# Row skewness on one core: a written order, slices of three and delayed copies exchanged for scheduled order, slices of two and copies at each block's end

## The chip, the cores and the metric

The kernel runs on one core of a Trainium2 chip. The metric is the device time of one execution in microseconds; the median of several executions is compared. The profile is one further execution, recorded by the hardware profiler.

## What is computed

For each of 1024 rows of 8192 float32 values the kernel returns the skewness:

```
mean = np.mean(x, axis=-1); std = np.std(x, axis=-1)
z = (x - mean) / (std + 1e-8)
out = np.mean(z ** 3, axis=-1)          # 1024 values
```

The kernel works with three sums per row, over x, x² and x³, and combines them: with S1, S2 and S3 as means, var = S2 - S1², and the result is (S3 - 3·S1·S2 + 2·S1³)·var^-1.5, which it evaluates as (S3 + (-3·S1)·(var + S1²/3))·var^-1.5 or in the equal form with S2 - (2/3)·S1².

## The kernel before, in words

The 1024 rows are eight blocks of 128 rows, one row per partition. Each block is loaded in column pieces called units (list `UNITS`, L18 to L27): blocks 0 to 3 in two units of 4096 columns, blocks 4 and 5 in three, block 6 in five, block 7 in eight small ones. All loads are issued by SyncE (L188) into a pool of eight buffers, so the ninth load and those after it wait until the buffer of the load eight places earlier has been released by its readers.

Every unit has three readers:

- ScalarE (ACT) squares it in slices, L195, with the running sum of squares as a by-product (accumulator column of `s2u`). The function `_slices` cuts a unit into parts of at most 2304 columns; units of at least 3584 columns in block 2 and later are cut into three parts of at most 1408.
- VectorE (DVE) multiplies each square by x, L200, with the sum of cubes as a by-product (column of `s3u`). It needs the square of the same slice, and the squares live in four buffers.
- TensorE (PE) transposes each 128 columns with an identity matrix and adds them up in PSUM (`tp`, L213), so that a block ends with one 128x128 matrix whose rows must still be summed. ScalarE copies it to SBUF (`copy_sums`, L112) and a matmul with a column of 1/8192 (`mean`, L115) yields the mean. In blocks 0 to 2, ScalarE sums 1024 columns of the first unit itself (L207).

The last slice of all keeps its square in PSUM (`sqps`) and its cube in another tile (`cube`).

The order on each engine is the order in which the program is written: `manual_schedule` (L52) takes the engines out of the scheduler's hands. A small table `todo`, filled by `at(b, k, fn)`, says which extra step stands after unit k of block b. The copy and the mean matmul of block b stand behind unit 0 of block b+1. The closing arithmetic of blocks 0 to 5 stands in block 6 (`first_sums`, `first_rest`), that of block 6 in block 7 (`mid_sums` L158, `mid_power` L163 to L166, `third_1` L169, `third_2` L172). The end for block 7, L223 to L241, is: copy, sum of `s2u`, mean, square of the mean, GpSimd (POOL) variance and power -1.5 (L232, L233), two Identity activations with a sum of `s3u` between them (L169, L226, L172), and one DVE operation with two per-row scalars that finishes the column (L238). Then SyncE looks at the last eight loads (L243) and stores 4 KB (L246).

Of the kernel before, what the change touches and what calls it, by code (L numbers as in the profile page):

```python
# [8 lines left out]
FP = mybir.dt.float32  # L9
AF = mybir.ActivationFunctionType  # L10
ALU = mybir.AluOpType
# [3 lines left out]
X_AXIS = mybir.AxisListType.X  # L15


UNITS = [  # L18
    [4096, 4096],
    [4096, 4096],  # L20
    [4096, 4096],
    [4096, 4096],
    [3072, 2944, 2176],
    [2944, 2688, 2560],
    [1664, 1536, 1664, 1792, 1536],
    [1024, 1152, 768, 1024, 1024, 1280, 1024, 896],
]  # L27
S1_ACT = {(0, 0): 1024, (1, 0): 1024, (2, 0): 1024}
SUB_MAX = 2304
SUB_WIDE = 1408  # L30
WIDE = 3584
X_BUFS = 8
SQ_BUFS = 4
EARLY = 6


def _slices(b, w):
    n = -(-w // (SUB_WIDE if b >= 2 and w >= WIDE else SUB_MAX))
    step = -(-w // n // 128) * 128
    return [(s, min(s + step, w)) for s in range(0, w, step)]  # L40

# [2 lines left out]
def kernel(  # L44
# [3 lines left out]
    out: bass.AP,  # L48
):
    nc = tc.nc  # L50
    eng = mybir.EngineType
    ctx.enter_context(tc.manual_schedule(  # L52
        engines={eng.PE, eng.Activation, eng.DVE, eng.Pool, eng.SP}))
    P = nc.NUM_PARTITIONS
    R, C = x.shape
    NB = R // P
    L = NB - 1
    F = EARLY
    inv_n = 1.0 / float(C)
    s_scale = float(C) ** -0.5  # L60
    third = (1.0 / 3.0) ** 0.5
    assert len(UNITS) == NB and all(sum(u) == C for u in UNITS) and F == L - 1
    nw = len(S1_ACT)
    assert sorted(b for b, _ in S1_ACT) == list(range(nw)) and nw <= F

# [2 lines left out]
    ov = out.rearrange("(p b) -> p b", b=NB)  # L68


    n_sl = [sum(len(_slices(b, w)) for w in u) for b, u in enumerate(UNITS)]
    K = max(n_sl)

    xpool = ctx.enter_context(tc.tile_pool(name="xp", bufs=X_BUFS))
    sqpool = ctx.enter_context(tc.tile_pool(name="sqp", bufs=SQ_BUFS))
# [1 line left out]
    psum = ctx.enter_context(tc.tile_pool(name="ps", bufs=2, space=bass.MemoryType.PSUM))  # L77
    psum1 = ctx.enter_context(tc.tile_pool(name="ps1", bufs=1, space=bass.MemoryType.PSUM))

    def small(name, n):  # L80
        return onep.tile([P, n], FP, tag=name, name=name)

    onesn = small("onesn", 1)
# [5 lines left out]
    s2u = small("s2u", NB * K)  # L89
    s3u = small("s3u", NB * K)  # L90
    nc.vector.memset(s2u, 0.0)
    nc.vector.memset(s3u, 0.0)
    s1a = small("s1a", nw)
    same = small("same", max(S1_ACT.values()))
    junk = small("junk", K)
    expo = small("expo", F)
    nc.gpsimd.memset(expo, -1.5)
    skew = small("skew", NB)
    s1ps = psum1.tile([P, NB], FP, tag="s1ps", name="s1ps")
    m1a = small("m1a", F)  # L100
    Tsb = [small(f"tsb{i}", P) for i in range(2)]
    tps = {}
    act, g, v = nc.scalar.activation, nc.gpsimd, nc.vector

    loads = []
    todo = {}

    def at(b, k, fn):
        todo.setdefault((b, k), []).append(fn)

    def copy_sums(b):
        nc.scalar.copy(out=Tsb[b % 2], in_=tps[b])  # L112

    def mean(b):
        nc.tensor.matmul(  # L115
            out=s1ps[:, b : b + 1], lhsT=Tsb[b % 2], rhs=onesn, start=True, stop=True
        )

    for b in range(L):
        at(b + 1, 0, lambda b=b: copy_sums(b))  # L120
        at(b + 1, 0, lambda b=b: mean(b))


    m2a, m3a, m1sqa, m1sq3a, nm1a, vara, rra = (
        small(f"{t}a", F) for t in ("m2", "m3", "m1sq", "m1sq3", "nm1", "var", "rr")
    )

    def first_sums():
        for dst, src in ((m2a, s2u), (m3a, s3u)):
            v.tensor_reduce(  # L130
                out=dst, in_=src[:, 0 : F * K].rearrange("p (b c) -> p b c", c=K),
                axis=X_AXIS, op=ALU.add,
            )
        nc.scalar.copy(out=m1a[:, nw:F], in_=s1ps[:, nw:F])
        act(out=m1sqa, in_=m1a, func=AF.Square)
        g.tensor_tensor(out=vara, in0=m2a, in1=m1sqa, op=ALU.subtract)  # L136
        g.tensor_tensor(out=rra, in0=vara, in1=expo, op=ALU.pow)  # L137

    def first_rest():
        act(out=m1sq3a, in_=m1a, func=AF.Square, scale=third)  # L140
        act(out=nm1a, in_=m1a, func=AF.Copy, scale=-3.0)
        g.tensor_tensor(out=m1sq3a, in0=m1sq3a, in1=vara, op=ALU.add)
        g.tensor_tensor(out=m1sq3a, in0=m1sq3a, in1=nm1a, op=ALU.mult)  # L143
        g.tensor_tensor(out=m3a, in0=m3a, in1=m1sq3a, op=ALU.add)  # L144
        g.tensor_tensor(out=skew[:, 0:F], in0=m3a, in1=rra, op=ALU.mult)  # L145

    at(F - 2, 0, lambda: v.tensor_tensor(  # L147
        out=m1a[:, 0:nw], in0=s1ps[:, 0:nw], in1=s1a, op=ALU.add))
    at(F, 1, first_sums)
    at(F, 2, first_rest)  # L150


    names = ("m2", "m3", "m1sq", "nm1", "var", "v3", "rr", "t")
    mid, end = ({t: small(f"{t}_{b}", 1) for t in names} for b in (F, L))

    def mid_sums():
        for t, src in (("m2", s2u), ("m3", s3u)):
            v.tensor_reduce(  # L158
                out=mid[t], in_=src[:, F * K : F * K + n_sl[F]], axis=X_AXIS, op=ALU.add
            )  # L160

    def mid_power():
        act(out=mid["m1sq"], in_=s1ps[:, F : F + 1], func=AF.Square)  # L163
        act(out=mid["nm1"], in_=s1ps[:, F : F + 1], func=AF.Copy, scale=-3.0)
        g.tensor_tensor(out=mid["var"], in0=mid["m2"], in1=mid["m1sq"], op=ALU.subtract)  # L165
        g.tensor_tensor(out=mid["rr"], in0=mid["var"], in1=expo[:, 0:1], op=ALU.pow)  # L166

    def third_1(o):
        act(out=o["v3"], in_=o["m1sq"], func=AF.Identity, scale=-2.0 / 3.0, bias=o["m2"])  # L169

    def third_2(o):
        act(out=o["t"], in_=o["v3"], func=AF.Identity, scale=o["nm1"], bias=o["m3"])  # L172

    at(L, 0, mid_sums)
    at(L, 1, mid_power)
    at(L, 4, lambda: third_1(mid))
    at(L, 5, lambda: third_2(mid))
    at(L, 5, lambda: g.tensor_tensor(  # L178
        out=skew[:, F : F + 1], in0=mid["t"], in1=mid["rr"], op=ALU.mult))

    for b, widths in enumerate(UNITS):
        tp = tps[b] = psum.tile([P, P], FP, tag="tp", name=f"tp_{b}")
        c0 = 0
        j = b * K
        for k, w in enumerate(widths):
            last_unit = b == L and k == len(widths) - 1
            xt = xpool.tile([P, w], FP, tag="x", name=f"x_{b}_{k}")
            loads.append(nc.sync.dma_start(out=xt, in_=xv[b, :, c0 : c0 + w]))  # L188
            c0 += w
            for s, e in _slices(b, w):  # L190
                if last_unit:
                    sq = psum1.tile([P, e - s], FP, tag="sqps", name="sqps")
                else:
                    sq = sqpool.tile([P, e - s], FP, tag="sq", name=f"sq_{b}_{k}_{s}")
                act(  # L195
                    out=sq, in_=xt[:, s:e], func=AF.Square, scale=s_scale,
                    accum_out=s2u[:, j : j + 1],
                )
                cube = sqpool.tile([P, e - s], FP, tag="sq", name="cube") if last_unit else sq
                v.scalar_tensor_tensor(  # L200
                    out=cube, in0=sq, scalar=1.0, in1=xt[:, s:e],
                    op0=ALU.mult, op1=ALU.mult, accum_out=s3u[:, j : j + 1],
                )
                j += 1
            w_act = S1_ACT.get((b, k), 0)
            if w_act:
                act(  # L207
                    out=same[:, 0:w_act], in_=xt[:, w - w_act : w], func=AF.Copy,
                    scale=inv_n, accum_out=s1a[:, b : b + 1],
                )  # L210
            n = (w - w_act) // P
            for c in range(n):
                nc.tensor.matmul(  # L213
                    out=tp, lhsT=xt[:, c * P : (c + 1) * P], rhs=ident,
                    start=(k == 0 and c == 0), stop=(c0 == C and c == n - 1),
                    is_transpose=True,
                )
            for fn in todo.pop((b, k), ()):
                fn()
    assert not todo  # L220


    o, p1 = end, s1ps[:, L : L + 1]  # L223

    def row_sum(out, src, n):
        act(out=junk[:, 0:n], in_=src[:, L * K : L * K + n], func=AF.Copy, accum_out=out)  # L226

    copy_sums(L)
    row_sum(o["m2"], s2u, n_sl[L])
    mean(L)  # L230
    act(out=o["m1sq"], in_=p1, func=AF.Square)  # L231
    g.tensor_tensor(out=o["var"], in0=o["m2"], in1=o["m1sq"], op=ALU.subtract)  # L232
    g.tensor_tensor(out=o["rr"], in0=o["var"], in1=expo[:, 0:1], op=ALU.pow)  # L233
    act(out=o["nm1"], in_=p1, func=AF.Copy, scale=-3.0)
    third_1(o)
    row_sum(o["m3"], s3u, n_sl[L] - 1)
    third_2(o)
    v.tensor_scalar(  # L238
        out=skew[:, L:NB], in0=s3u[:, j - 1 : j], scalar1=o["t"], scalar2=o["rr"],
        op0=ALU.add, op1=ALU.mult,  # L240
    )  # L241

    seen = nc.sync.nop()  # L243
    for ld in loads[-8:]:
# [32 lines left out]
```

## Time and profile before

| | us |
|---|---|
| Median of 4 runs | 91.13 (91.04 to 91.15) |
| The profiled execution's own time | 91.19 |
| Its span, first to last instruction | 89.4 |
| DVE busy, share of the span | 73.5, 82% |
| ACT busy | 72.6, 81% |
| PE busy | 65.5, 73% |
| POOL busy | 13.7, 15% |
| Read from HBM | 33.55 MB, 375 GB/s over the span |

The time outside the span is 1.79 us. "Idle before" of an instruction is the time its engine stood still in front of it; the arrow names what ended that. A slice on ACT or DVE is one long instruction and a short accumulator read (80 to 190 ns), which overlaps the start of the next slice: the distance between the starts of two slices is shorter than the sum of their durations.

### The profile page before, as it was taken

How to read it: one execution, taken by the hardware profiler on the slowest of the kernel's cores; microseconds unless marked ns; L12 is line 12 of the kernel's file. 1: busy time of each engine (PE TensorE's matmuls, PEld its weight loads, DVE VectorE, ACT ScalarE, POOL GpSimd, SP SyncE). 2: the span in 40 equal slices, each digit the busy share in tenths (PEclk: the TensorE clock that was granted, in tenths of full speed). 3: DMA queues.
4: the chain of work that ended last, by engine and by line, in shares of the span. 5: the costliest groups of instructions: out<-in, count | busy, mean ns of one | idle time of the engine just before them, and what ended most of it. 6: DMA issues, size and time to landing. Idle time of an engine off the chain costs nothing.

```text
span 89.4 us, 1405 instructions
## 1 busy us (share of the span) xinstructions
PE 65.5 (73%) x504; PEld 61.0 (68%) x504; DVE 73.5 (82%) x97; ACT 72.6 (81%) x120; POOL 13.7 (15%) x18
## 2 busy tenths in 40 slices
PE   0003999792797925999999699489897889897810
PEld 0003999691796915999999598479796778865710
DVE  1000498989989497999989999999999999999980
ACT  6003999599990999979799999499899989998960
POOL 3000000000000000000000000000000089999730
PEclk9999999999958997599999999999999999999999
DMA  5899999999999999999999999999999999995000
GB/s 117 337 411 425 455 425 411 455 433 411 447 440 389 455 440 396 455 418 422 425 419 401 443 420 413 427 424 408 411 419 415 418 405 405 414 410 230 10 0 2
DMA packets 4038, 33.64 MB, mean 376 GB/s; under 512 B 576, under 2 KB 576, under 8 KB 2240
## 3 DMA queue, kind: packets, MB, share of 16 engines
q1 hardware_dynamic: 4032, 33.56, 90.2%
q8 instruction: 4, 0.07, 0.3%
q14 instruction: 2, 0.02, 0.0%
HBM read 33.55 MB, written 0.00 MB: 375 GB/s over the span
## 4 chain that ended last, share of the span: by engine, by line
DMA 53%; DVE 26%; ACT 7%; issue 7%; SPq 4%; PE 0%; DVEq 0%; ACTq 0%
DMA x<-in_x_dram 53%; DVE sq L200 25%; ACT sq L195 4%; SPq L188 4%; ACT sqps L195 1%; ACT t L172 1%; PE s1ps L115 0%; DVE skew L238 0%; ACT v L169 0%; ACT junk L226 0%; ACT m1sq L231 0%; ACT tsb L112 0%; DVE m2a L130 0%; DVE m3a L130 0%; DVE m1a L147 0%
## 5 line engine op out<-in xcount | busy, mean ns | idle before, releaser
L200 DVE SCALAR_TENSOR_TENSOR sq<-sq,x 128x1408 f32<-128x1408 f32 (+9 forms) x43 | 71.7, 1720 | 12.5 <-ACT sq L195 12.4
L195 ACT ACTIVATE sq<-x 128x1408 f32<-128x1408 f32 (+9 forms) x43 | 62.3, 1451 | 13.1 <-DMA x<-in_x_dram 12.3
L213 PE MATMUL tp<-ident,x 128*128 128x128 f32 x488 | 63.4, 292 | 12.4 <-DMA x<-in_x_dram 12.2
L213 PEld LDWEIGHTS tp<-ident,x 128*128 128x128 f32 x488 | 59.5, 153 | 15.2 <-issue 8.1
L136 POOL TENSOR_TENSOR vara<-m2a,m1sqa 128x6 f32<-128x6 f32 x1 | 1.8, 1812 | 70.3 <-DVE m3a L130 70.3
L115 PEld LDWEIGHTS s1ps<-onesn,tsb 128*128 128x128 f32 x16 | 2.6, 203 | 9.3 <-ACT tsb L112 9.3
L115 PE MATMUL s1ps<-onesn,tsb 128*128 128x1 f32 x16 | 3.2, 267 | 7.6 <-ACT tsb L112 7.6
L195 ACT ACTIVATION_READ_ACCUMULATOR sq<-x 128x1 f32 x43 | 8.0, 186 | 0.0
L200 DVE DVE_READ_ACCUMULATOR sq<-sq,x 128x1 f32 x43 | 3.5, 82 | 0.0
L137 POOL TENSOR_TENSOR rra<-vara,expo 128x6 f32<-128x6 f32 x1 | 3.1, 3133 | 0.1
L207 ACT ACTIVATE same<-x 128x1024 f32<-128x1024 f32 x3 | 3.1, 1041 | 0.0
L112 ACT COPY tsb<-tp 128x128 f32<-128x128 f32 x8 | 1.9, 243 | 0.0
L86 ACT ACT_TABLE_LOAD x1 | 1.3, 1283 | 0.7 <-PEq L261 0.7
L166 POOL TENSOR_TENSOR rr<-var,expo 128x1 f32<-128x1 f32 x1 | 1.4, 1426 | 0.1
L144 POOL TENSOR_TENSOR m3a<-m3a,m1sq3a 128x6 f32<-128x6 f32 x1 | 1.3, 1331 | 0.1
L165 POOL TENSOR_TENSOR var<-m,m1sq 128x1 f32<-128x1 f32 x1 | 1.2, 1173 | 0.0
L200 DVE SCALAR_TENSOR_TENSOR cube<-sqps,x 128x896 f32<-128x896 f32 x1 | 1.1, 1087 | 0.0
L143 POOL TENSOR_TENSOR m1sq3a<-m1sq3a,nm1a 128x6 f32<-128x6 f32 x1 | 1.1, 1066 | 0.1
L178 POOL TENSOR_TENSOR skew<-t,rr 128x1 f32<-128x1 f32 x1 | 1.0, 977 | 0.1
L195 ACT ACTIVATE sqps<-x 128x896 f32<-128x896 f32 x1 | 0.9, 900 | 0.0
L145 POOL TENSOR_TENSOR skew<-m3a,rra 128x6 f32<-128x6 f32 x1 | 0.8, 802 | 0.1
L172 ACT ACTIVATE t<-v,m,nm 128x1 f32<-128x1 f32 x2 | 0.8, 380 | 0.0
(36 smaller groups left out, 7.5 us busy)
## 6 DMA issues: line engine op xcount, KB each, us to landing
x<-in_x_dram SPq DMA_DIRECT2D x8, 2048.0 KB, 23.4
x<-in_x_dram SPq DMA_DIRECT2D x2, 1472.0 KB, 29.6
x<-in_x_dram SPq DMA_DIRECT2D x4, 512.0 KB, 8.4
x<-in_x_dram SPq DMA_DIRECT2D x2, 832.0 KB, 18.2
x<-in_x_dram SPq DMA_DIRECT2D x1, 1536.0 KB, 32.7
x<-in_x_dram SPq DMA_DIRECT2D x2, 768.0 KB, 15.9
x<-in_x_dram SPq DMA_DIRECT2D x1, 1344.0 KB, 25.0
x<-in_x_dram SPq DMA_DIRECT2D x1, 1280.0 KB, 23.0
```

The lines of the kernel that those rows point to most:

```text
L86: nc.scalar.activation(out=tiny, in_=onesn, func=AF.Square)
L112: nc.scalar.copy(out=Tsb[b % 2], in_=tps[b])
L115: nc.tensor.matmul(out=s1ps[:, b : b + 1], lhsT=Tsb[b % 2], rhs=onesn, start=True, stop=True)
L136: g.tensor_tensor(out=vara, in0=m2a, in1=m1sqa, op=ALU.subtract)
L137: g.tensor_tensor(out=rra, in0=vara, in1=expo, op=ALU.pow)
L166: g.tensor_tensor(out=mid["rr"], in0=mid["var"], in1=expo[:, 0:1], op=ALU.pow)
L172: act(out=o["t"], in_=o["v3"], func=AF.Identity, scale=o["nm1"], bias=o["m3"])
L188: loads.append(nc.sync.dma_start(out=xt, in_=xv[b, :, c0 : c0 + w]))
L195: act(out=sq, in_=xt[:, s:e], func=AF.Square, scale=s_scale, accum_out=s2u[:, j : j + 1],)
L200: v.scalar_tensor_tensor(out=cube, in0=sq, scalar=1.0, in1=xt[:, s:e], op0=ALU.mult, op1=ALU.mult, accum_out=s3u[:, j : j + 1],)
L207: act(out=same[:, 0:w_act], in_=xt[:, w - w_act : w], func=AF.Copy, scale=inv_n, accum_out=s1a[:, b : b + 1],)
L213: nc.tensor.matmul(out=tp, lhsT=xt[:, c * P : (c + 1) * P], rhs=ident, start=(k == 0 and c == 0), stop=(c0 == C and c == n - 1), is_transp ...
```

## The change

The manual order and the `todo` table go; a scheduler orders the engines. `UNITS` of blocks 4 to 7 are cut anew, with 27 loads as before. The rule for three slices goes, so units of 4096 and 3584 columns are cut in two again: 36 slices in place of 43. The copy and the mean matmul of a block stand directly behind its last unit. The closing of blocks 0 to 5 stands whole behind block 5 (`close_first_blocks`). Blocks 6 and 7 each get their numerator from a chain of six activations (`close_on_act`), of which the last puts a correction into one more column of `s3u`; the power for both blocks is one POOL operation of two columns at the very end, and DVE sums `s3u` of both blocks and multiplies. The look of SyncE at the last eight loads and the store are the same lines in both.

```diff
-    [3072, 2944, 2176],
-    [2944, 2688, 2560],
-    [1664, 1536, 1664, 1792, 1536],
-    [1024, 1152, 768, 1024, 1024, 1280, 1024, 896],
+    [3584, 2304, 2304],
+    [2304, 2304, 2048, 1536],
+    [1664, 1792, 1920, 1664, 1152],
+    [1024, 1024, 1152, 1280, 1408, 1152, 1152],
...
-    n = -(-w // (SUB_WIDE if b >= 2 and w >= WIDE else SUB_MAX))
+    n = -(-w // SUB_MAX)
...
-    ctx.enter_context(tc.manual_schedule(
-        engines={eng.PE, eng.Activation, eng.DVE, eng.Pool, eng.SP}))
...
-    for b in range(L):
-        at(b + 1, 0, lambda b=b: copy_sums(b))
-        at(b + 1, 0, lambda b=b: mean(b))
...
+    def close_on_act(b):
...
+        yield act(out=junk, in_=s2u[:, b * K : b * K + K], func=AF.Copy, accum_out=m2)
+        yield act(out=m1sq, in_=p1, func=AF.Square)
+        yield act(out=var, in_=m1sq, func=AF.Identity, scale=-1.0, bias=m2)
+        yield act(out=nm1, in_=p1, func=AF.Copy, scale=-3.0)
+        yield act(out=v3, in_=m1sq, func=AF.Identity, scale=1.0 / 3.0, bias=var)
+        yield act(
+            out=s3u[:, b * K + K - 1 : b * K + K], in_=v3, func=AF.Identity, scale=nm1
+        )
...
+            if k > 0:
+                next(pending, None)
+                next(pending, None)
+        tsb = Tsb[b % 2]
+        nc.scalar.copy(out=tsb, in_=tp)
+        nc.tensor.matmul(out=s1ps[:, b : b + 1], lhsT=tsb, rhs=onesn, start=True, stop=True)
+        if b == F - 2:
+            nc.vector.tensor_tensor(
+                out=m1a[:, 0:nw], in0=s1ps[:, 0:nw], in1=s1a, op=ALU.add
+            )
+        if b == F - 1:
+            close_first_blocks()
+        if b >= F:
+            pending = close_on_act(b)
+    for _ in pending:
+        pass
+    rr = small("rr2", NB - F)
+    nc.gpsimd.tensor_tensor(out=rr, in0=var2, in1=expo[:, 0 : NB - F], op=ALU.pow)
+    num = small("num2", NB - F)
+    nc.vector.tensor_reduce(
+        out=num, in_=s3u[:, F * K :].rearrange("p (b c) -> p b c", c=K), axis=X_AXIS, op=ALU.add
+    )
+    nc.vector.tensor_tensor(out=skew[:, F:NB], in0=num, in1=rr, op=ALU.mult)
```

## The prediction, made before the changed kernel was run

> **What bounds the kernel now.** I read the page's slices first, then the chain of waits, then the timelines of ACT, DVE and PE. The slices say whether the loads are ever the thing that pauses.
>
> ```profile
> DVE  1000498989989497999989999999999999999980
> ACT  6003999599990999979799999499899989998960
> PEclk9999999999958997599999999999999999999999
> DMA  5899999999999999999999999999999999995000
> ```
>
> DMA is full from the second slice to the 36th, and stops some 6 us before the end. So the loads set when the last data arrive, and the time behind the last data is the kernel's tail. DVE is full from the middle on: it is almost as slow as the loads. The clock has two dents. The chain of waits gives the end:
>
> ```profile
> 4.17 39.56 DMA x<-in_x_dram
> 43.81 1.48 ACT sq L195 x2
> 45.31 2.65 DVE sq L200 x3
> ...
> 73.50 7.80 DMA x<-in_x_dram
> 81.38 1.25 ACT sq L195
> ...
> 84.06 0.93 ACT sqps L195 x2
> 85.00 0.16 ACT tsb L112
> ...
> 85.20 0.40 PE s1ps L115 x2
> ...
> 86.34 0.40 ACT t L172
> ...
> 86.83 0.27 DVE skew L238
> ```
>
> Two loads land at 43.73 and 81.30 by it. Between them lie 30,848 columns of loads (blocks 4 to 7 without their last 1920), so 37.57 us / 30,848 = 1.218 ns a column; the last load lands near 81.30 + 1920 x 1.218 ns = 83.64. PE's weight loads start on it at 83.67. After that: square, copy, mean, a few activations, one DVE operation. DVE's own sums end at 86.40, only 0.43 us ahead of L238, so two lines run almost level into the end: **ACT's tail** and **DVE's work**.
>
> The timeline shows how a load starts the engines, and PE's view what its clock does:
>
> ```profile
> 22.79 1.91 ACT L195 ACTIVATE sq<-x 128x2048 f32<-128x2048 f32 x1
> 29.12 1.38 ACT L195 ACTIVATE sq<-x 128x1408 f32<-128x1408 f32 x1 [2.43 <-DMA x<-in_x_dram]
> 45.31 1.63 DVE L200 SCALAR_TENSOR_TENSOR sq<-sq,x 128x1408 f32<-128x1408 f32 x1 [0.31 <-ACT sq L195]
> ```
>
> ```profile
> 22.94 0.38 PE L115 MATMUL s1ps<-onesn,tsb 128*128 128x1 f32 x2 [2.34 <-ACT tsb L112]
> 23.19 5.36 PE L213 MATMUL tp<-ident,x 128*128 128x128 f32 x32
> ```
>
> The line at 45.31 is the last wait of DVE for a square before the end (later pauses are 0.05 to 0.35 us). 32 transposes take 5.36 us at 23.19, while 23 in a stretch at full clock take 2.73 (0.112 us each after 0.27 for the first): a window of 24.2 to 27.6 us shows a granted clock of 0.50, as does 34.4 to 37.9. Both follow PE pauses of over 2.3 us.
>
> **The change, part by part.**
>
> *Loads.* Still 27, still 19 of them in blocks 4 to 7, with the same bytes. The last load therefore lands at 83.64 again. The buffers are released a little later, but the last loads were issued 5 to 8 us ahead of landing (6.4 us for the last, of which the DMA's own turn is about 1.1), so a delay of half a microsecond is covered.
>
> *Seven fewer slices.* A DVE slice of 2048 columns starts 2.22 us before the next (12.31 to 14.53), one of 1024 takes 1.15 (77.10 to 78.25): 1.045 ns a column and 0.08 us a slice. ACT by the same (1.90 and 1.04): 0.84 ns and 0.18 us. Seven slices are 0.56 us of DVE, 1.3 us of ACT.
>
> *The first slice of a wide unit is longer.* DVE must wait for it: 2.04 us from ACT's start to DVE's with 2048 columns (8.06 to 10.10), 1.50 with 1408 (43.81 to 45.31). So the last restart of DVE goes from 45.31 to 45.85.
>
> DVE's line before: 45.31, plus 36,864 columns x 1.045 = 38.52, plus 27 slices x 0.08 = 2.16, plus its small operations (0.07 + 0.23 + 0.13) = 86.42; the trace has 86.40. After: 45.85 + 38.52 + 22 x 0.08 + 0.30 = 86.43. The two edits cancel.
>
> The Trainium skill speaks on both sides of this. "VectorE: DVE Perf Modes", in its TRN2 errata section, charges every instruction a fixed latency and recommends large tiles; "Perfetto Trace Analysis", section Optimizing Scalar/DVE Operations, says that breaking up instructions can let work finish sooner where an engine causes bubbles on others. The first alone would make the change a gain of about half a microsecond, the second a loss like that at the restart; the rows above weigh them as equal.
>
> *Copies behind the block's own last unit.* The copy now waits for that unit's last transpose, and the next block's squares stand behind it on ACT. In blocks 0, 1 and 3 PE is done before or about when the next load lands. In block 2 the second unit lands near 33.9; PE at half clock needs 5.36 us for it, to about 39.4, the copy ends at 39.55, and block 3's first square starts at 39.6 instead of 38.91. DVE then starts block 3 at 41.6, is busy to 46.05, and the restart at 45.85 becomes 46.05. If the half clock does not fall there the price is 0; I take 0.2, so DVE ends its cubes at 86.43 to 86.63.
>
> The page "TensorE: Matmul & The Clock Gate" (What's actually happening) describes a gate that halves the clock after an idle window of about 3.4 us, free-running, so that its place varies by run. The two dents here are that long. By the page the 0.2 us is a matter of phase; the sum holds either end.
>
> *Closings.* Behind block 5 ACT has copy, mean, a copy of means and three activations in a row, some 1.2 us; DVE is about 3 us of work behind ACT there. Behind block 6 the built program puts copy, sum of `s2u` and the square of the mean in front of block 7's first square (copy to square of the mean is 0.72 us at 84.90 to 85.62), and three activations more behind it (0.6). The second square of block 7 is then ready near 78.4, and DVE needs it at 78.5 to 78.7. Covered, with 0.1 to 0.3 us to spare; if not, the loss is 0.1 to 0.4. POOL's first chain starts earlier and is done long before the end.
>
> *The tail.* The last unit has 1152 columns instead of 896, but the one before it lands 1.40 us earlier and ACT is free: the last square starts at 83.72 and ends at 84.87 (before: 84.90, as ACT was late then). PE has nine transposes, 9 x 0.112 + 0.27 from 83.7: 84.98, so the copy starts at 85.0, 0.1 later. The mean's square starts 0.72 behind it, 85.72. Then each step waits for the one before: variance at 85.92 (0.20, as 85.62 to 85.82), v3 at 86.25, the correction at 86.58 (0.29 + 0.04 each), done at 86.97 (0.39, as L172), against 86.73. DVE follows 0.10 later: a reduction (0.15 to 0.20 by L158 and L130), and, where L238 stood alone, a product (0.15 by L147, 0.1 for the dependence): 86.97 + 0.10 + 0.16 + 0.09 + 0.15 = 87.47, against 87.10. That is +0.37. Cubes at 86.63 stay under it. POOL's power of two columns starts at 86.25 and took 0.54 for one column at the end (L233): 86.8, covered by the reduction; bounds below. The store behind it is the same.
>
> **Sum.** 91.19 + 0.37 = 91.56 for the profiled execution, which stood 0.06 above the median: 91.5 against 91.13.
>
> **Rivals.**
>
> *A slow operation or a half clock on the longer line.* Against 0.54, POOL's power took 1.43 us for one column at 81.88 (L166) and 3.13 for six (L137), all while DVE read two SBUF tiles; interpolated, 1.8 for two. At 1.43 it ends at 87.68 and the product at 87.9 (+0.8); at 1.8, +1.2. For it: the slow rows are the majority. Against: the last cube takes its square from PSUM, as when 0.54 was seen. The other form is a half clock under block 3's second unit: copy 1.7 us late, DVE 0.7 later, 91.8. Time 91.7 to 92.3. It decides once power or cubes pass 87.07.
>
> *The tail's additions are hidden.* If the three dependent activations cost 0.20 each as L169 to L226 do, and PE is not behind, the correction ends near 86.7 and reduction plus product add 0.1: 91.0 to 91.3, no change.
>
> *Faster: the loads' stretch does not recur.* Blocks' units start 4.9 us apart (12.91, 17.80, 22.79), but 22.79 to 29.12 is 6.33: one load landed 1.4 us late, and all later landings kept that. If in the new program nothing delays that load, every later landing, and with them both lines into the end, is up to 1.4 us earlier: 90.1. For it: the delay is no part of the kernel's own loads. Against: loads up to there are identical, and PE's instruction stream, the longest, is nearly so. It would show as ACT starting block 2 at 27.7 instead of 29.1.
>
> **How the numbers follow.** Forecast case 0.62, 91.3 to 91.7. Slow operation or half clock 0.17, 91.7 to 92.3. Hidden tail 0.14, 91.0 to 91.3. Faster 0.07, 90.1 to 90.9. A measurement here tells about 0.2%, 0.18 us. Slower than that: the forecast case and the slow rival, 0.79; same 0.14; faster 0.07. The range leaves out the faster case and the top of the slow one: 91.1 to 92.2.
>
> **What would show it.** Right: last load landing near 83.6; DVE's cubes ending 86.4 to 86.7; correction done near 87.0; product ending near 87.5. Step by step: ACT's wait at the copy of block 2 to 39.4; a DVE restart at 45.85 or 46.05; 36 slices with about 0.56 us less DVE time. Wrong: a landing well off 83.6, DVE pauses in block 7 (the closing of block 6 was not covered), a product that waits for POOL, or the DVE line ending later than ACT's correction.

## The result: 0.17 us slower, and the profile after

| | before | after |
|---|---|---|
| Median, us | 91.16 (69 runs) | 91.33 (45 runs) |
| Ratio | 1 | 1.0019, 95% interval 1.0014 to 1.0024 |
| The profiled execution's own time, us | 91.19 | 91.49 |
| Its span, us | 89.4 | 89.7 |

The interval excludes no change, and the size is at the edge of what one comparison of this kernel can tell. The change takes eight slices away, not seven as stated above: the kernel before has 44, since its last one, `cube`, is listed apart from the other 43. DVE's busy time fell from 73.5 to 72.7 us with it. The slices of the page of the changed kernel, as above:

```profile
DVE  1000498989999199895999999999999999999980
...
PEclk9999999999859996699999999999999999999997
DMA  3999999999999999999999999999999999994000
```

DMA is full over the same stretch. DVE has deeper holes, the 1 in slice 14 and the 5 in slice 19 (near 30 and 41 us: the first squares of blocks 2 and 3, wider and later), and none after them. The last part of the chain of waits of the changed kernel (start, length, what):

```profile
3.40 30.70 DMA x<-in_x_dram
...
34.14 5.38 PE tp L169 x32
...
39.71 2.02 ACT sq L151 x2
...
41.74 2.19 DVE sq L156
...
76.40 7.36 DMA x<-in_x_dram
...
83.78 1.26 ACT sqps L151 x2
...
85.04 0.28 ACT tsb L178
...
85.36 0.40 PE s1ps L179 x2
...
86.31 0.30 ACT v L130
...
86.64 0.30 ACT s3u L131
...
86.96 0.18 DVE num L193
...
87.23 0.16 DVE skew L196
```

PE's transposes of block 2 have entered the chain, with 5.38 us for 32 of them, and ACT's first square of block 3 stands behind them at 39.71. At the end the last square starts as the data land, at 83.78; in the kernel before it started at 83.97, 0.30 us behind PE's first weight load on the same data (83.67), with L172 between two of the last squares. ACT and DVE of the kernel before at the end:

```profile
82.65 0.37 ACT L172 ACTIVATE t<-v,m,nm 128x1 f32<-128x1 f32 x1
...
83.97 0.90 ACT L195 ACTIVATE sqps<-x 128x896 f32<-128x896 f32 x1
...
86.83 0.27 DVE L238 TENSOR_SCALAR skew<-s3u,t,rr 128x1 f32<-128x1 f32 x1 [0.35 <-ACT t L172]
```

Around the end, PE, ACT, POOL and DVE of the changed kernel:

```profile
84.73 0.27 PE L169 MATMUL tp<-ident,x 128*128 128x128 f32 x1
...
85.04 0.27 ACT L178 COPY tsb<-tp 128x128 f32<-128x128 f32 x1
...
86.35 0.70 POOL L191 TENSOR_TENSOR rr<-var,expo 128x2 f32<-128x2 f32 x1 [7.54 <-ACT var L128]
...
86.96 0.17 DVE L193 TENSOR_REDUCE num<-s3u 128x2 f32<-128x16 f32 x1 [0.17 <-ACT s3u L131]
```

DVE stood still for 0.17 us in front of its reduction, waiting for ACT's correction: its cubes are done before ACT's chain is. The last transpose ends at 85.00, and the copy starts 0.04 later: PE, not ACT, now sets the copy.

### The profile page after: what moved, and what is told of

It reads as the page before. It is cut to its first block, busy times and chain, and to the rows that moved or that the text cites. A ratio compares the mean times of both kernels' runs of the same rounds, so it can differ in the third digit from the quotient of the medians.

```text
span 89.7 us, 1369 instructions
## 1 busy us (share of the span) xinstructions
PE 66.4 (74%) x504; PEld 60.8 (68%) x504; DVE 72.7 (81%) x80; ACT 72.2 (81%) x106; POOL 11.3 (13%) x14
## 4 chain that ended last, share of the span: by engine, by line
DMA 57%; DVE 21%; PE 6%; ACT 5%; issue 4%; SPq 3%; DVEq 0%
DMA x<-in_x_dram 57%; DVE sq L156 20%; PE tp L169 6%; SPq L144 3%; ACT sq L151 2%; ACT sqps L151 1%; PE s1ps L179 0%; ACT v L130 0%; ACT s3u L131 0%; ACT tsb L178 0%; ACT var L128 0%; DVE num L193 0%; ACT m1sq L127 0%; DVE skew L196 0%; ACT nm L129 0%
## 5 line engine op out<-in xcount | busy, mean ns | idle before, releaser
L156 DVE SCALAR_TENSOR_TENSOR sq<-sq,x 128x2048 f32<-128x2048 f32 (+9 forms) x35 | 70.6, 2070 | 13.6 <-ACT sq L151 13.6
L169 PE MATMUL tp<-ident,x 128*128 128x128 f32 x488 | 64.0, 292 | 16.1 <-DMA x<-in_x_dram 15.9
L169 PEld LDWEIGHTS tp<-ident,x 128*128 128x128 f32 x488 | 59.2, 153 | 19.6 <-DMA x<-in_x_dram 11.2
L151 ACT ACTIVATE sq<-x 128x2048 f32<-128x2048 f32 (+9 forms) x35 | 60.6, 1733 | 9.5 <-DMA x<-in_x_dram 9.0
L151 ACT ACTIVATION_READ_ACCUMULATOR sq<-x 128x1 f32 x35 | 6.5, 186 | 0.0
L156 DVE DVE_READ_ACCUMULATOR sq<-sq,x 128x1 f32 x35 | 2.9, 82 | 0.0
L114 POOL TENSOR_TENSOR m1sq3a<-m1sq3a,vara 128x6 f32<-128x6 f32 x1 | 1.9, 1871 | 0.1
L191 POOL TENSOR_TENSOR rr<-var,expo 128x2 f32<-128x2 f32 x1 | 0.7, 701 | 7.5 <-ACT var L128 7.5
L156 DVE SCALAR_TENSOR_TENSOR cube<-sqps,x 128x1152 f32<-128x1152 f32 x1 | 1.4, 1350 | 0.0
L151 ACT ACTIVATE sqps<-x 128x1152 f32<-128x1152 f32 x1 | 1.1, 1137 | 0.1
```

The source lines that it names most:

```text
L114: g.tensor_tensor(out=m1sq3, in0=m1sq3, in1=var, op=ALU.add)
L151: nc.scalar.activation(out=sq, in_=xt[:, s:e], func=AF.Square, scale=s_scale, accum_out=s2u[:, j : j + 1],)
L156: nc.vector.scalar_tensor_tensor(out=cube, in0=sq, scalar=1.0, in1=xt[:, s:e], op0=ALU.mult, op1=ALU.mult, accum_out=s3u[:, j : j + 1],)
L169: nc.tensor.matmul(out=tp, lhsT=xt[:, c * P : (c + 1) * P], rhs=ident, start=(k == 0 and c == 0), stop=(c0 == C and c == n - 1), is_transp ...
```

## The experiments

Landings wander from profile to profile: PE's first weight load on the last unit stands between 83.63 and 83.97 in the thirteen profiles. So the table counts from there. The first three columns add up to the fourth; they come from one profile each. The last is the ratio of the times, of 4 to 12 runs of each experiment against 17 to 35 runs of the kernel before in the same comparison.

| kernel | to the copy | copy to end of ACT's chain | to end of DVE's last operation | sum, us | time against before (95% interval) |
|---|---|---|---|---|---|
| before | 1.23 | 1.83 | 0.37 | 3.43 | 1 |
| changed | 1.24 | 1.89 | 0.46 | 3.59 | 1.0019 (1.0014 to 1.0024) |
| before, new ends | 1.03 | 1.88 | 0.48 | 3.39 | 1.0001 (0.9991 to 1.0011) |
| before, two slices | 1.22 | 1.83 | 0.39 | 3.44 | 1.0007 (0.9997 to 1.0018) |
| before, own copies | 1.21 | 1.83 | 0.37 | 3.41 | 1.0002 (0.9993 to 1.0012) |
| before, new loads | 1.38 | 1.83 | 0.35 | 3.56 | 1.0015 (1.0004 to 1.0026) |
| changed, old ends | 1.67 | 1.83 | 0.68 | 4.18 | 1.0095 (1.0081 to 1.0110) |
| changed, last load 896 | 1.06 | 1.86 | 0.86 | 3.78 | 1.0038 (1.0026 to 1.0051) |
| changed, old loads | 1.03 | 1.89 | 0.63 | 3.55 | 1.0006 (0.9994 to 1.0017) |
| before, step of L172 earlier | 1.03 | 1.84 | 0.39 | 3.26 | 0.9978 (0.9965 to 0.9991) |
| changed, last load 1024 | 1.13 | 1.89 | 0.51 | 3.53 | 1.0006 (0.9995 to 1.0017) |
| changed, second load 1152 | 1.24 | 1.89 | 0.67 | 3.80 | 1.0040 (1.0026 to 1.0055) |
| changed, three slices | 1.24 | 1.88 | 0.47 | 3.59 | 1.0008 (0.9995 to 1.0021) |

The sums follow the times: +0.16 against a measured 0.17 for the change, -0.17 against -0.20 for the step of L172, +0.37 against +0.36 for the exchanged loads. In the other rows they differ by at most 0.09 us, and by 0.12 with the old ends. No run changes the scheduling alone, so what the written order is worth by itself is not shown.

**Theories.** *Tail*: ACT's closing chain and the DVE operations behind it set the end, DVE's cubes stand just under it. *Cubes*: the wide slices and the copies move DVE's restart, and the cubes set the end.

### Before, with the new closings of blocks 6 and 7

```diff
-    at(L, 0, mid_sums)
-    at(L, 1, mid_power)
...
+    steps = close_on_act(F)
...
+    for k in (1, 2, 3):
+        at(L, k, two_steps)
...
     copy_sums(L)
...
     mean(L)
+    for _ in close_on_act(L):
+        pass
```

`two_steps` takes two of the six activations; power, reduction and product stand at the end as in the change.

> The kernel before with only the closings of blocks 6 and 7 of the changed kernel: three activations that wait for each other, one power of two columns, a reduction and a product on DVE. Theory tail (ACT's closing chain and the two DVE operations behind it set the end, DVE's cubes stand just under it): copy at 84.9 as before, correction done near 86.8, product done near 87.23 against 87.10; 0.10 to 0.25 us slower than before. Theory cubes (the wide slices and the copies move DVE's last restart, and the cubes set the end): no change, within 0.05 us, since slices and copies are those of before.

No change was measured. The trace shows that ACT's chain is 0.05 and DVE's end 0.11 us longer, as the tail theory says, but the copy comes 0.20 earlier: block 6's last activation (L172) no longer stands between the last squares on ACT. The expectation had the copy where it was and missed this gain.

### Before, with the wide units in two slices

```diff
-    n = -(-w // (SUB_WIDE if b >= 2 and w >= WIDE else SUB_MAX))
+    n = -(-w // SUB_MAX)
```

> The kernel before with only the wide units of blocks 2 and 3 in two slices instead of three. Theory tail: DVE's last restart goes from 45.3 to 45.85 and the cubes end 0.4 us later, near 86.8, which is level with ACT's chain (86.73): 0.05 to 0.15 us slower than before, less than the shift of the cubes. Theory cubes: the whole shift is seen, 0.4 us slower.

0.07% slower, an interval that just includes no change, and well short of 0.4 us. DVE's last restart was at 45.91 (45.85 forecast), and its cubes ended 0.39 us later than before, 0.23 counted from the last landing. Its last operation started 0.12 us behind ACT's chain, without a wait: the two lines met.

### Before, with each copy behind its own block

```diff
-        at(b + 1, 0, lambda b=b: copy_sums(b))
-        at(b + 1, 0, lambda b=b: mean(b))
+        at(b, len(UNITS[b]) - 1, lambda b=b: copy_sums(b))
+        at(b, len(UNITS[b]) - 1, lambda b=b: mean(b))
```

> The kernel before with only the copy and the mean matmul of each block behind its own last unit. ACT should wait at the copy of block 2 until near 39.5, if PE is at half clock there, and start block 3 at 39.7 instead of 38.9; DVE then is busy through its restart at 45.3, to 45.7. Theory tail: cubes near 86.8, 0.05 to 0.15 us slower. Theory cubes: 0.4 us slower. If the half clock is absent in block 2: no change in both.

No change. The half clock was not under block 2's second unit in this execution, so ACT's copy there started at 38.00 without a wait: the last clause of the expectation applies. How much the wait costs when it happens is not told by this run; the kernel with three slices below has the wait.

### Before, with the new loads

```diff
-    [3072, 2944, 2176],
...
-    [1024, 1152, 768, 1024, 1024, 1280, 1024, 896],
+    [3584, 2304, 2304],
...
+    [1024, 1024, 1152, 1280, 1408, 1152, 1152],
```

> The kernel before with only the loads of blocks 4 to 7 cut as in the changed kernel (last load 1152 columns instead of 896). The last load lands at 83.6 as before. Theory tail: nine transposes instead of seven put the copy at 85.0 instead of 84.9 and the end 0.1 us later. Theory cubes: the cubes end 0.1 to 0.2 us later, and so does the kernel. The trace tells which of the two DVE's last operation waited for.

0.15% slower, nearly the whole of the change's loss. ACT of this kernel around the last load:

```profile
83.78 0.37 ACT L172 ACTIVATE t<-v,m,nm 128x1 f32<-128x1 f32 x1
84.06 1.11 ACT L195 ACTIVATE sqps<-x 128x1152 f32<-128x1152 f32 x1
...
85.20 0.24 ACT L112 COPY tsb<-tp 128x128 f32<-128x128 f32 x1
```

L172 stands in front of the last square here, and that square is 1152 columns wide: the copy starts at 85.20, 1.38 us behind PE's first weight load, against 1.23 before. DVE's last operation waited 0.35 us for ACT, so this is ACT's line. From this a third theory, *units*: the width of the last load is what costs. L172 in front of the last square is part of the 1.38, and the changed kernel does not have it there.

### The changed kernel with the old closings

```diff
-    def close_on_act(b):
...
+    def mid_steps():
...
-        if b >= F:
-            pending = close_on_act(b)
+        if b == F:
+            pending = mid_steps()
```

`mid_steps` holds the sums, powers and activations of `mid_sums` to `third_2`; the end is that of L223 to L241.

> The changed kernel with the closings of blocks 6 and 7 of the kernel before. The theory of the prediction (three activations in a row and two DVE operations cost 0.2 us and more): the loss of the change goes, 0 to 0.05 us off the kernel before. Theory units, formed after the new closings alone cost nothing in the kernel before and the new loads alone cost 0.14 us: the loss stays, 0.1 to 0.2 us slower than before, since the last load of 1152 columns is still there.

0.95% slower, which neither theory had. The old closing stands in another place on ACT here. `mid_steps` hands out one step behind each unit of block 7, so the activations of L169 and L172 (L125 and L128 here) are written behind the third and fourth unit instead of the fifth and sixth, and the scheduler put both in front of the third unit's square:

```profile
78.97 0.30 ACT L125 ACTIVATE v<-m1sq,m 128x1 f32<-128x1 f32 x1 [0.72 <-DVE m L132]
...
80.86 1.36 DVE L167 SCALAR_TENSOR_TENSOR sq<-sq,x 128x1152 f32<-128x1152 f32 x1 [0.78 <-ACT sq L162]
```

ACT stood still for 0.72 us at a small activation that needs sums that DVE makes only when it gets there; the squares behind it came late, and DVE then waited 0.78 us for one. The kernel thus says nothing on the price of the ends by themselves. It shows what a closing costs where it stands in front of squares.

### The changed kernel with a last load of 896

```diff
-    [1024, 1024, 1152, 1280, 1408, 1152, 1152],
+    [1024, 1152, 1280, 1408, 1408, 1024, 896],
```

> The changed kernel with block 7 cut into 1024, 1152, 1280, 1408, 1408, 1024 and 896 columns: as many loads, the last one 896 instead of 1152. Theory units: the last copy starts 0.2 us earlier behind the last landing; the cubes of DVE stay where they are, 0.17 us under the reduction, and catch the rest: 0.10 to 0.15 us faster than the changed kernel, so 0 to 0.1 us slower than before. Theory of the prediction (closings): 0.05 us faster than the changed kernel at most.

0.38% slower. The copy came 0.18 us earlier, as the units theory says, but DVE waited 0.39 us for the second square of block 7 and ended last. In the built program L131 had moved in front of that square. Two things were changed at once here; the next kernels take them apart.

### The changed kernel with the old loads

```diff
-    [3584, 2304, 2304],
...
-    [1024, 1024, 1152, 1280, 1408, 1152, 1152],
+    [3072, 2944, 2176],
...
+    [1024, 1152, 768, 1024, 1024, 1280, 1024, 896],
```

> The changed kernel with the loads of the kernel before in blocks 4 to 7, wide units in two slices. Theory units in its simple form (only the last load's width counts): 0.15 us faster than the changed kernel, level with before. Theory two lines (ACT's tail and DVE's cubes both stand close, whichever ends last counts): 39 slices instead of 36 on DVE from the late restart put the cubes near 87.0 instead of 86.7, the product ends near 87.5, and the kernel is as slow as the changed one or slower, 0.15 to 0.35 us above before, with DVE's reduction no longer waiting for ACT.

0.06% above before, with an interval (-0.06% to +0.17%) that includes no change, as the simple units theory says, and just reaches the lower edge of the two-lines theory. The traced sum is 0.12 us above before, so the two are not told apart by the time. The two-lines sum had the cubes near 87.0; they ended at 86.65, since PE had no half clock in block 2 (its copy started at 37.85) and DVE restarted at 45.88. Its reduction did follow the cubes without a wait, as the two-lines theory says.

### Before, with one step of block 6's closing earlier

```diff
-    at(L, 5, lambda: third_2(mid))
-    at(L, 5, lambda: g.tensor_tensor(
+    at(L, 4, lambda: third_2(mid))
+    at(L, 4, lambda: g.tensor_tensor(
```

> The kernel before with one step of the closing of block 6, the activation at L172 and its product on POOL, one unit earlier in block 7, so that it no longer stands between two of the last three squares on ACT. Two lines: the last square starts at its landing instead of 0.25 us behind it, the copy starts 0.14 us earlier (PE then is last), ACT's chain ends near 86.6, still above the cubes at 86.5: 0.10 to 0.15 us faster than before. If the cubes set the end: no change.

0.22% faster than before (0.09% to 0.35%), and so faster than both kernels; 91.14 us against 91.33 in that comparison. The 0.20 us are more than the 0.10 to 0.15 expected, as the copy came 0.20 us earlier instead of 0.14. ACT and DVE of this kernel at the end:

```profile
83.75 0.90 ACT L195 ACTIVATE sqps<-x 128x896 f32<-128x896 f32 x1
...
84.68 0.26 ACT L112 COPY tsb<-tp 128x128 f32<-128x128 f32 x1
...
86.13 0.39 ACT L172 ACTIVATE t<-v,m,nm 128x1 f32<-128x1 f32 x1
```

```profile
85.39 1.08 DVE L200 SCALAR_TENSOR_TENSOR cube<-sqps,x 128x896 f32<-128x896 f32 x1
...
86.63 0.28 DVE L238 TENSOR_SCALAR skew<-s3u,t,rr 128x1 f32<-128x1 f32 x1
```

The square starts at 83.75 instead of 83.97, the copy at 84.68 instead of 84.90, and L238 at 86.63 instead of 86.83, with no wait left that the profile shows: both lines now end together.

### The changed kernel with a last load of 1024

```diff
-    [1024, 1024, 1152, 1280, 1408, 1152, 1152],
+    [1024, 1024, 1152, 1280, 1408, 1280, 1024],
```

> The changed kernel with the last two loads of block 7 cut into 1280 and 1024 columns instead of 1152 and 1152; the order on ACT at the start of block 7 stays. ACT's chain starts 0.1 us earlier behind the last landing, DVE's cubes stay. If the last load's width sets the loss: 0.05 to 0.11 us faster than the changed kernel, 0.05 to 0.15 us slower than before, with DVE's reduction near 86.85 and almost no wait in front of it. If DVE's cubes set it: no change against the changed kernel.

0.06% above before (interval -0.05% to +0.17%). The copy stands 1.13 us behind PE's first weight load, against 1.24 with 1152 columns and 1.03 with 896 (in three kernels above): 0.10 to 0.11 us for each 128 columns, one transpose. Where ACT is free, PE's last transposes set the copy, which starts 0.04 us behind them in all of these. DVE's reduction started at 86.78, without a wait: the cubes became last, so 0.06 us of the 0.11 showed in the sum.

### The changed kernel with its second and third load of block 7 exchanged

```diff
-    [1024, 1024, 1152, 1280, 1408, 1152, 1152],
+    [1024, 1152, 1024, 1280, 1408, 1152, 1152],
```

> The changed kernel with the second and third load of block 7 exchanged (1152, then 1024). The scheduler then puts the last step of block 6's closing (L131) in front of the second square of block 7 instead of behind it, as in the kernel with the last load of 896. If that closing is what DVE ran out of work for there: DVE stands still 0.4 us in front of that slice, the cubes end near 87.0, and the kernel is 0.2 to 0.35 us slower than the changed one, with the last load as wide as in it. If it was the widths of the last loads: as fast as the changed kernel.

0.40% slower than before and, by the two ratios, 0.19 us slower than the changed kernel, just below the first clause. ACT and DVE of this kernel:

```profile
77.51 0.29 ACT L131 ACTIVATE s3u<-v,nm 128x1 f32<-128x1 f32 x1
```

```profile
77.35 1.22 DVE L156 SCALAR_TENSOR_TENSOR sq<-sq,x 128x1024 f32<-128x1024 f32 x1
...
78.98 1.36 DVE L156 SCALAR_TENSOR_TENSOR sq<-sq,x 128x1152 f32<-128x1152 f32 x1 [0.41 <-ACT sq L151]
...
87.11 0.17 DVE L193 TENSOR_REDUCE num<-s3u 128x2 f32<-128x16 f32 x1
```

In the changed kernel L131 stands at 78.45, behind that square. One activation of 0.29 us in front of a square instead of behind it, and a square 128 columns wider, together stop DVE for 0.41 us; what each is worth is not shown. The cubes then end last and the reduction follows them without a wait.

### The changed kernel with three slices

```diff
-def _slices(w):
-    n = -(-w // SUB_MAX)
+def _slices(w, wide=False):
+    n = -(-w // (1408 if wide else SUB_MAX))
...
-            for s, e in _slices(w):
+            for s, e in _slices(w, b >= 2 and w >= 3584):
```

> The changed kernel with the wide units of blocks 2, 3 and 4 in three slices again. ACT's wait for the copy of block 2 stays, so DVE starts block 3 near 41.2 instead of 41.7 and has three to five more slices to pay (0.08 us each): the cubes end 0 to 0.2 us earlier. If ACT's chain sets the end of the changed kernel: no change, 0.1 to 0.2 us slower than before. If the wide slices set it: the loss goes.

The sum is that of the changed kernel to 0.01 us (3.59), though DVE started block 3 at 40.99 instead of 41.74. The line of its reduction:

```profile
86.79 0.17 DVE L193 TENSOR_REDUCE num<-s3u 128x2 f32<-128x18 f32 x1 [0.18 <-ACT s3u L131]
```

DVE waits for ACT's correction as in the changed kernel. The lead of 0.75 us did not reach the end: more slices and pauses for squares (0.18 us in front of the slice at 79.73) used it up, and the cubes end 2.90 us behind PE's first weight load on the last unit, against 2.91 in the changed kernel. So the wide slices do not set the end; what earlier cubes would win, this run does not say. The measured ratio, 1.0008, has an interval from -0.05% to +0.21%: it includes no change against before as well as the whole loss of the change.

## Why the prediction was right, and what was mis-sized

**The mechanism held.** Two lines run almost level into the end, ACT's chain just above DVE's cubes. In the changed kernel the reduction waits 0.17 us for ACT; with three slices it waits 0.18; and where ACT's chain comes earlier (the last load of 1024, the old loads) the cubes come up as last. The size did not hold: the tail grew by less than half of what I had, and all three of its terms were too large.

**The landing.** Forecast 83.64, found at 83.76. Over all profiles PE's first weight load on the last unit moved by 0.3 us, without a clear pattern by loads, so nothing ties the 0.13 us between the two shown profiles (83.67 and 83.80) to the change. The profiled executions differ by 0.30 us, which is these 0.13 and 0.16 of tail; the medians differ by 0.17.

**DVE's line.** Forecast: block 3 begins on DVE at 41.6, is busy to 46.05, cubes end at 86.43 to 86.63. Found: 41.74, 46.18 and 86.71. The copy of block 2 waited for PE to 39.54 (39.4 forecast), as that unit landed at 34.1 instead of 33.9. From 46.18 on, the forecast's own sum gives 86.76, so the cost of slices and columns held to 0.05 us. It counts slices from the restart on, 27 and 22, and the slip in their whole number (44, not 43) does not touch it. The 86.40 and 86.71 are the starts of the last accumulator read, which ends 0.08 us later: DVE's margin in the kernel before was the 0.35 us that the profile shows in front of L238, not 0.43.

**The tail, by terms.** Against before, with both counted from the landing, I had +0.10 for the copy, +0.14 for ACT's chain, +0.13 for DVE's last operations; the two profiles show +0.01, +0.06 and +0.09. So the tail grew by 0.16 instead of 0.37 us. The three terms were too large by 0.09, 0.08 and 0.04, for these reasons:

- *Nine transposes.* I wrote 9 x 0.112 + 0.27, but the rule that I had taken from the trace says 0.112 each after the first, which makes 8 x 0.112 + 0.27 = 1.17; the trace shows 1.20. One transpose was counted twice.
- *The correction.* I took 0.39 us from L172, whose scale and addend are both per-row values. In L131 only the scale is one, and it took 0.29; as each step stood 0.02 us later than forecast behind the copy, 0.08 of the 0.10 remains.
- *DVE's end.* Reduction and product took 0.46 from ACT's end to theirs, not 0.50.

**Where the loss sits.** In the tail as forecast, but not as I split it. The wider last load adds two transposes and 0.24 us of square; against that, the new closing of block 6 no longer holds the last square back, which is worth 0.20 (before with new ends). So the +0.01 at the copy is the balance of two shifts of about 0.2 us; the longer chain and the extra DVE operation remain. The loads alone cost 0.15% in the kernel before; the new ends alone cost nothing, as their 0.16 us at the end are paid by the 0.20 at the copy; the changed kernel with old loads stands at 1.0006, though its interval reaches 1.0017. By the times the loads are the larger part, and the prediction gave the wider last load 0.1 of 0.37. By the traces a return to the old loads wins only 0.04 of the 0.16 us, as the cubes then end last. How the loss divides between loads and ends thus stays open.

**The covers.** Block 6's closing was to be covered with 0.1 to 0.3 us to spare. For the second square of block 7 it was: ACT ended it at 78.45, and DVE took it at 78.68 without a wait. The third, which stands behind L131, was late by little: ACT ended it at 79.79, and DVE's slice started at 79.91, 1.23 us behind the one before it instead of 1.15. The kernel with the exchanged loads shows what DVE loses where the cover is gone, 0.41 us (0.1 to 0.4 forecast), about half of which reached the kernel's time.

**The rivals.** POOL's power took 0.70 for two columns, ended at 87.05 and was covered by 0.18 us. The half clock stayed off block 3. The stretch of the loads recurred: ACT's first squares stand at 22.83 and 29.27, 6.44 apart. The hidden tail came nearest of the three, with 91.0 to 91.3; the changed kernel's median, 91.33, lies at the border between it and the forecast case. Its conditions did not hold, though: the dependent activations start 0.33 us apart, not 0.20, the correction ends at 86.93, not 86.7, and PE is last in front of the copy.

The page "Perfetto Trace Analysis" of the Trainium skill, section Optimizing Scalar/DVE Operations, says that breaking up instructions may let work complete sooner where the engine is not saturated but causes bubbles on others. Here two slices in place of three cost 0.07% in the kernel before (at most 0.18%), and in the changed one no difference was measured. The fixed cost of each instruction, of which "VectorE: DVE Perf Modes" speaks in its TRN2 errata section, stands on the other side; here it is 0.08 us a slice on DVE.

## What to carry to other kernels

Behind the last landing, write down who is last at each step (the square's engine, the transposes, the chain, the other line's backlog): a small operation in front of the last square was worth 0.2 us here, and moving it one unit up beat both kernels. Where two lines end within 0.2 us of each other, a gain on one is cut off by the other, so a single edit's measured effect is less than its shift. A closing step belongs where its inputs already exist and where the engine behind it has work in store; in a scheduled program a change of widths can move such a step in front of a square.

## What the runs showed of the hardware that I had not expected

The place of PE's half clock changed between executions whose instructions up to there are the same. One window of the changed kernel, and of the one with the exchanged loads of block 7 (PEclk is the third number from the end):

```profile
34.60:38.00 3.40, 3.40 (x20) 3.40 (x19) 3.00 (x3) 3.40 (x4) 0.00 (x0) 0.56 1.01 429
```

```profile
34.60:38.00 3.40, 3.22 (x30) 2.98 (x28) 3.01 (x3) 3.40 (x5) 0.00 (x0) 1.00 1.03 439
```

With 0.56 in this window the 32 transposes of block 2's second unit took 5.37 us and the copy started at 39.54; with 1.00 they took 3.71 and it started at 37.95. Every such stretch between 20 and 40 us in the thirteen profiles is 3.4 us long, and the two of the kernel before, like the two of the changed one, start 10.2 us apart, three times that length. That agrees with the free-running window of the Trainium skill's page "TensorE: Matmul & The Clock Gate" (What's actually happening). The page puts an idle window of about 3.4 us in front of the half clock; here a PE pause of 2.07 us was enough (at 34.14 in the changed kernel), while one of 2.34 us (at 34.48 in the kernel before with two slices) brought none. On this point the measurement decides.

The half clock moved DVE's restart by 0.2 us. Whether it moved the end of a kernel is not shown: in the kernel with the last load of 1024, where the cubes end last, block 2's copy had waited for PE to 39.28.

POOL's times for one operation spread widely: its power of six columns took 3.26 us in the changed kernel and 1.34 in the one with the old closings. DVE was multiplying beside both, but the fast one had started at 72.31, in a pause of DVE from 72.30 to 72.40, the slow one at 72.45, 0.09 us into a slice. What decides it stays open.
